# Two broadcast VectorE products and three ScalarE products per output tile in place of eight and eight

## The chip, the core and the metric

The kernel runs on one core of a Trainium2 chip. The metric is the device time of one execution in microseconds (us); lower is better. Three parts of the core matter here: VectorE (DVE in the profile) and ScalarE (ACT), which do the arithmetic, and the 16 DMA engines, which move data between the chip's main memory (HBM) and the on-chip memory (SBUF). DMA transfers are issued from the instruction queue of SyncE (SP) and from the one of ScalarE; each of the two has its own DMA queue, q1 for SP and q10 for ScalarE.

## The reference

Each token's row of 512 numbers is written out twice, once multiplied by its first weight and once by its second. The expert indices are not used.

```python
batch, seq, hidden = x.shape            # 16, 1024, 512, float32
k = expert_indices.shape[-1]            # 2
x_expanded = x[:, :, np.newaxis, :].repeat(k, axis=2)
weights = expert_weights[..., np.newaxis]
return (x_expanded * weights).astype(np.float32)
```

So 33.5 MB are read, 67.1 MB are written, and there is one multiplication for each number written.

## The kernel before, in words

The 16384 tokens are cut into 8 groups of 2048. A group lies in SBUF as one x_tile of 128 partitions with 16 tokens each (4096 KB), so that each partition reads one contiguous stretch of 32 KB. The x pool has two buffers (line 41). A group's results fill two output tiles, o_tile, of 8 tokens by 2 weights by 512 numbers (4096 KB each); the output pool has four buffers (line 42). All weights lie in one w_tile of 128 partitions by 256 numbers.

Lines 54 and 55 issue eight small loads of weights from SP, one for each group. The function load (lines 69 to 77) issues the 4096 KB load of one x_tile from ScalarE's queue (line 76). Lines 79 and 80 load groups 0 and 1; after group i has been worked on, line 109 asks for group i + 2, which takes the buffer of group i and therefore has to wait until every product that reads it is done.

The loop over the 8 tokens of an output tile makes two products for each token: weight 1 on ScalarE (lines 91 to 95) and weight 0 on VectorE (lines 97 to 103). Each reads 512 numbers in each partition and multiplies them by one weight per partition. After the eighth token SP issues the store of the whole o_tile (lines 105 to 108). A store waits for both engines' products; a product into a recycled o_tile waits until the store of four output tiles earlier has landed.

Waits between engines and the order of instructions in each engine's queue are made by the Tile framework: it orders an engine's instructions itself, so that a load's place in ScalarE's queue need not be the place of its line in the source. In the trace the load of line 76 stands in ScalarE's queue behind the first product of the next group. Below, stores and output tiles are counted from 0 to 15, groups and their loads from 0 to 7.

Of the kernel before, what the change touches and what calls it, by code (L numbers as in the profile page):

```python
# [1 line left out]

# [4 lines left out]


@with_exitstack
def kernel(  # L10
    ctx: ExitStack,
    tc: tile.TileContext,
    x: bass.AP,
    expert_indices: bass.AP,
    expert_weights: bass.AP,
    out: bass.AP,
):
    nc = tc.nc

    batch, seq, hidden = x.shape  # L20
    k = expert_weights.shape[-1]
    P = nc.NUM_PARTITIONS
    ntok = batch * seq
    assert ntok % P == 0
    A_TOTAL = ntok // P

    f32 = mybir.dt.float32
    row = k * hidden
    TX = 16
    TO = 8  # L30


    groups = [[16], [16], [16], [16], [16], [16], [16], [16]]
    assert sum(sum(g) for g in groups) == A_TOTAL

    xf = x.rearrange("b s h -> (b s) h")
    of = out.rearrange("b s k h -> (b s) (k h)")
    wf = expert_weights.rearrange("b s k -> (b s) k")

    w_pool = ctx.enter_context(tc.tile_pool(name="w_pool", bufs=1))  # L40
    x_pool = ctx.enter_context(tc.tile_pool(name="x_pool", bufs=2))
    o_pool = ctx.enter_context(tc.tile_pool(name="o_pool", bufs=4))

    w_tile = w_pool.tile([P, A_TOTAL * k], f32)

    def rows(of_all, done, T):
        return of_all[done * P : (done + T) * P, :].rearrange(
            "(p a) n -> p (a n)", a=T
        )

    weights = []
    for group in groups:
        weights.append((sum(n for _, n in weights), sum(group)))
    for at, T in weights:
        nc.sync.dma_start(out=w_tile[:, at * k : (at + T) * k], in_=rows(wf, at, T))

    tiles = []
    done = 0
    for group in groups:
        T = sum(group)  # L60
        a0 = 0
        for n in group:
            tiles.append((done, T, a0, n))
            a0 += n
        done += T

    loaded = []

    def load(i):
        if i >= len(tiles):  # L70
            return
        done, T, a0, n = tiles[i]
        x_tile = x_pool.tile([P, TX * hidden], f32)
        cols = rows(xf, done, T)[:, a0 * hidden : (a0 + n) * hidden]
        for lo, hi in [(0, P)]:
            nc.scalar.dma_start(out=x_tile[lo:hi, : n * hidden], in_=cols[lo:hi, :])  # L76
        loaded.append(x_tile)

    for i in range(2):
        load(i)  # L80
    for i, (done, T, a0, n) in enumerate(tiles):
        x_tile = loaded[i]
        outr = rows(of, done, T)
        for t in range(n):
            if t % TO == 0:
                o_tile = o_pool.tile([P, TO * row], f32)
            for kk in range(k):
                c = (done + a0 + t) * k + kk
                o = t % TO * row + kk * hidden
                if kk == 1:  # L90
                    nc.scalar.mul(  # L91
                        out=o_tile[:, o : o + hidden],
                        in_=x_tile[:, t * hidden : (t + 1) * hidden],
                        mul=w_tile[:, c : c + 1],
                    )
                    continue
                nc.vector.tensor_scalar(  # L97
                    out=o_tile[:, o : o + hidden],
                    in0=x_tile[:, t * hidden : (t + 1) * hidden],
                    scalar1=w_tile[:, c : c + 1],  # L100
                    scalar2=None,
                    op0=mybir.AluOpType.mult,
                )
            if (t + 1) % TO == 0:
                nc.sync.dma_start(
                    out=outr[:, (a0 + t + 1 - TO) * row : (a0 + t + 1) * row],
                    in_=o_tile,
                )
        load(i + 2)

# [1 line left out]
_INS = ['x', 'expert_indices', 'expert_weights']  # L112
_OUTS = [((16, 1024, 2, 512), 'float32')]


# [23 lines left out]
```

## Time and profile before

| | |
|---|---|
| median of 5 runs | 240.12 us (240.06 to 240.21) |
| the profiled execution's own time | 240.09 us |
| its span, first to last instruction | 238.3 us |
| VectorE busy | 52.0 us in 128 instructions, mean 481 ns |
| ScalarE busy | 81.3 us, of which 80.1 us are 128 products, mean 708 ns |
| bytes over DMA | 100.81 MB, mean 423 GB/s |
| a store, from issue to landing | 21.6 to 57.1 us, median 48.4 us |
| a load of x, from issue to landing | 12.5 to 23.3 us, median 23.2 us |
| a load of weights, from issue to landing | 3.9 to 22.3 us, median 21.0 us |

The time lies 1.8 us above the span: work around the program that the trace of the program does not contain. A DMA's issue is only its order; its packets run later, and it counts as landed when the last of them has arrived. A row of instructions gives the engine, the operation, output and inputs, the shape, the count, the busy time and the mean of one; "idle before" is how long the engine stood still before such instructions, and what ended it. A row of a stretch of time gives its length, the busy time of each engine with the number of instructions begun in it, the clock of TensorE (not used here), the mean busy share of the 16 DMA engines and their rate. Packets are counted at their start, so in short stretches a share can lie above 1.

### The profile page before, as it was taken

How to read it: one execution, taken by the hardware profiler on the slowest of the kernel's cores; microseconds unless marked ns; L12 is line 12 of the kernel's file. 1: busy time of each engine (PE TensorE's matmuls, PEld its weight loads, DVE VectorE, ACT ScalarE, POOL GpSimd, SP SyncE). 2: the span in 40 equal slices, each digit the busy share in tenths (PEclk: the TensorE clock that was granted, in tenths of full speed). 3: DMA queues.
4: the chain of work that ended last, by engine and by line, in shares of the span. 5: the costliest groups of instructions: out<-in, count | busy, mean ns of one | idle time of the engine just before them, and what ended most of it. 6: DMA issues, size and time to landing. Idle time of an engine off the chain costs nothing.

```text
span 238.3 us, 384 instructions
## 1 busy us (share of the span) xinstructions
DVE 52.0 (22%) x128; ACT 81.3 (34%) x129; POOL 0.2 (0%) x4
## 2 busy tenths in 40 slices
DVE  0073900045005004050230503214040235000000
ACT  1079960076107007080260803417043256200000
POOL 0000000000000000000000000000000000000000
DMA  6999999999999999999999999999999999999996
GB/s 267 442 442 362 435 435 424 413 424 429 440 440 440 437 440 440 435 429 429 429 418 429 429 440 440 440 435 440 440 435 424 435 429 418 429 429 440 440 440 264
DMA packets 4610, 100.81 MB, mean 423 GB/s; under 512 B 1536, under 2 KB 1536, under 8 KB 1536
## 3 DMA queue, kind: packets, MB, share of 16 engines
q1 hardware_dynamic: 3456, 67.24, 65.6%
q10 hardware_dynamic: 1152, 33.55, 33.1%
q14 instruction: 2, 0.02, 0.0%
HBM read 33.69 MB, written 67.11 MB: 423 GB/s over the span
## 4 chain that ended last, share of the span: by engine, by line
DMA 60%; another core or an unknown queue 12%; ACT 12%; ACTq 1%; issue 0%
DMA out_dram<-o_tile 41%; DMA x_tile<-in_x_dram 18%; ACT o_tile L91 12%; DMA w_tile<-in_expert_weights_dram 2%; ACTq L76 0%; ACTq L134 0%; ACTq L91 0%
## 5 line engine op out<-in xcount | busy, mean ns | idle before, releaser
L91 ACT ACTIVATE o_tile<-x_tile,w_tile 128x512 f32<-128x512 f32 x128 | 80.1, 708 | 117.4 <-DMA out_dram<-o_tile 96.3
L97 DVE TENSOR_SCALAR o_tile<-x_tile,w_tile 128x512 f32<-128x512 f32 x128 | 52.0, 481 | 150.2 <-DMA out_dram<-o_tile 115.7
L91 ACT ACT_TABLE_LOAD x1 | 1.3, 1283 | 5.0 <-DMA w_tile<-in_expert_weights_dram 5.0
L123 POOL MEMSET const-bfloat16-1.0<- 128x1 bf16 x1 | 0.1, 101 | 0.0
L123 POOL MEMSET const-uint8-127<- 128x1 uint8 x1 | 0.1, 101 | 0.0
L123 POOL MEMSET const-float32-0.0<- 128x1 f32 x1 | 0.1, 98 | 0.2 <-issue 0.2
L123 POOL MEMSET const-float32-1.0<- 128x1 f32 x1 | 0.1, 98 | 0.0
## 6 DMA issues: line engine op xcount, KB each, us to landing
out_dram<-o_tile SPq DMA_DIRECT2D x16, 4096.0 KB, 48.4
x_tile<-in_x_dram ACTq DMA_DIRECT2D x8, 4096.0 KB, 23.2
w_tile<-in_expert_weights_dram SPq DMA_DIRECT2D x8, 16.0 KB, 21.0
```

Of the source, the lines that this page charges most:

```text
L91: nc.scalar.mul(out=o_tile[:, o : o + hidden], in_=x_tile[:, t * hidden : (t + 1) * hidden], mul=w_tile[:, c : c + 1],)
L97: nc.vector.tensor_scalar(out=o_tile[:, o : o + hidden], in0=x_tile[:, t * hidden : (t + 1) * hidden], scalar1=w_tile[:, c : c + 1], scala ...
L123: nc = _bacc.Bacc("TRN2", target_bir_lowering=False, num_devices=1)
```

## The change

The products of one output tile are given out differently. Of the 16 products (8 tokens, 2 weights), VectorE takes both weights of tokens 0 to 4 in one instruction of 5120 numbers per partition, and weight 0 of tokens 5 to 7 in a second one of 1536. Both are products of two tensors: x is read with a broadcast over the weights, and the weights with a broadcast over the 512 numbers. ScalarE keeps weight 1 of tokens 5 to 7, three products in the same form as before. Over the 16 output tiles VectorE has 32 instructions in place of 128, ScalarE 48 products in place of 128; in numbers per partition, VectorE goes from 4096 to 6656 for each output tile, ScalarE from 4096 to 1536. Loads, stores, tiles and buffers stay as they are.

```diff
     w_tile = w_pool.tile([P, A_TOTAL * k], f32)
+    ws = w_tile.rearrange("p (a k) -> p a k", k=k)
...
-        for t in range(n):
-            if t % TO == 0:
-                o_tile = o_pool.tile([P, TO * row], f32)
-            for kk in range(k):
-                c = (done + a0 + t) * k + kk
-                o = t % TO * row + kk * hidden
-                if kk == 1:
-                    nc.scalar.mul(...)
-                    continue
-                nc.vector.tensor_scalar(...)
+        xs = x_tile.rearrange("p (t h) -> p t h", h=hidden)
+        for t0 in range(0, n, TO):
+            o_tile = o_pool.tile([P, TO * row], f32)
+            os = o_tile.rearrange("p (t k h) -> p t k h", k=k, h=hidden)
+            c0 = done + a0 + t0
+
+            def product(t, kk):
+
+                m, s = t.stop - t.start, kk.stop - kk.start
+                nc.vector.tensor_tensor(
+                    out=os[:, t, kk, :],
+                    in0=xs[:, t0 + t.start : t0 + t.stop, :]
+                    .unsqueeze(2)
+                    .to_broadcast([P, m, s, hidden]),
+                    in1=ws[:, c0 + t.start : c0 + t.stop, kk]
+                    .unsqueeze(3)
+                    .to_broadcast([P, m, s, hidden]),
+                    op=mybir.AluOpType.mult,
+                )
+
+            split = TO - 3
+            product(slice(0, split), slice(0, k))
+            product(slice(split, TO), slice(0, k - 1))
+            for t in range(split, TO):
+                o = t * row + (k - 1) * hidden
+                c = (c0 + t) * k + k - 1
+                nc.scalar.mul(
                     out=o_tile[:, o : o + hidden],
-                    in0=x_tile[:, t * hidden : (t + 1) * hidden],
-                    scalar1=w_tile[:, c : c + 1],
-                    scalar2=None,
-                    op0=mybir.AluOpType.mult,
+                    in_=xs[:, t0 + t, :],
+                    mul=w_tile[:, c : c + 1],
                 )
-            if (t + 1) % TO == 0:
-                nc.sync.dma_start(
-                    out=outr[:, (a0 + t + 1 - TO) * row : (a0 + t + 1) * row],
-                    in_=o_tile,
-                )
+            nc.sync.dma_start(
+                out=outr[:, (a0 + t0) * row : (a0 + t0 + TO) * row], in_=o_tile
+            )
         load(i + 2)
```

More of the change, by code (lines that the diff above doesn't have):

```diff
@@ L83 @@
         outr = rows(of, done, T)
-        for t in range(n):
-            if t % TO == 0:
-                o_tile = o_pool.tile([P, TO * row], f32)
-            for kk in range(k):
-                c = (done + a0 + t) * k + kk
-                o = t % TO * row + kk * hidden
-                if kk == 1:
[L91 to L94, printed above, removed]
-                    )
-                    continue
-                nc.vector.tensor_scalar(
+        xs = x_tile.rearrange("p (t h) -> p t h", h=hidden)
@@ L98 @@
                     out=o_tile[:, o : o + hidden],
-                    in0=x_tile[:, t * hidden : (t + 1) * hidden],
-                    scalar1=w_tile[:, c : c + 1],
-                    scalar2=None,
-                    op0=mybir.AluOpType.mult,
-                )
-            if (t + 1) % TO == 0:
-                nc.sync.dma_start(
-                    out=outr[:, (a0 + t + 1 - TO) * row : (a0 + t + 1) * row],
-                    in_=o_tile,
-                )
+                    in_=xs[:, t0 + t, :],
```

## The prediction

> **What bounds the kernel now.** I read first the page's busy times, its row of DMA shares and its table of DMA queues.
>
> ```profile
> DVE 52.0 (22%) x128; ACT 81.3 (34%) x129; POOL 0.2 (0%) x4
> ...
> DMA  6999999999999999999999999999999999999996
> ...
> q1 hardware_dynamic: 3456, 67.24, 65.6%
> q10 hardware_dynamic: 1152, 33.55, 33.1%
> ```
>
> The arithmetic engines are a quarter and a third busy. The two DMA queues together fill 65.6 + 33.1 = 98.7% of 16 engines for 238.3 us, that is 235.2 us. Only 3.1 us of the span are without DMA work. The next view says where they are: busy time, DMA share and rate by stretch.
>
> ```profile
> 0.00:2.00 2.00, 0.00 (x0) 0.00 (x0) 0.20 (x4) 1.00 0.40 104
> 2.00:4.00 2.00, 0.00 (x0) 0.00 (x0) 0.00 (x0) 1.00 0.73 281
> 4.00:20.00 16.00, 6.43 (x16) 8.00 (x12) 0.00 (x0) 1.00 1.01 434
> 20.00:24.00 4.00, 0.24 (x1) 3.44 (x7) 0.00 (x0) 1.00 1.07 334
> 24.00:48.00 24.00, 6.87 (x18) 10.42 (x18) 0.00 (x0) 1.00 1.01 434
> ...
> 160.21:204.00 43.79, 13.04 (x32) 20.04 (x32) 0.00 (x0) 1.00 1.01 436
> 204.00:236.00 32.00, 0.00 (x0) 0.00 (x0) 0.00 (x0) 1.00 1.00 432
> 236.00:238.30 2.30, 0.00 (x0) 0.00 (x0) 0.00 (x0) 1.00 0.00 0
> ```
>
> The missing time is in the first 4 us (1.2 + 0.5 us), before any product can start, and in the last 2.3 us, after the last packet has started. In between the share is 1. The rate of 334 GB/s in 20 to 24 us is no idle stretch either: there the queue of SP works off the weights, which come in packets of 128 bytes. So the kernel is bound by DMA from end to end, at 432 GB/s, 9.7 us for each 4096 KB.
>
> Third, the waits: who waited for whom.
>
> ```profile
> DVE o_tile L97 <- DMA out_dram<-o_tile: 115.7, 11, 13.8
> ACT o_tile L91 <- DMA out_dram<-o_tile: 96.3, 11, 12.0
> DVE o_tile L97 <- DMA x_tile<-in_x_dram: 34.5, 3, 17.1
> ACT o_tile L91 <- DMA x_tile<-in_x_dram: 21.1, 3, 13.6
> ```
>
> Columns: who waited for what, us in all, times, the longest. Both engines stand still until a store has freed an output buffer, 11 times, and until x is there, three times: arithmetic waits for DMA. Last, the timeline at the start, the one place where DMA does depend on the products.
>
> ```profile
> 13.29 9.91 ACT L91 ACTIVATE o_tile<-x_tile,w_tile 128x512 f32<-128x512 f32 x16 [6.96 <-DMA x_tile<-in_x_dram]
> 13.29 6.43 DVE L97 TENSOR_SCALAR o_tile<-x_tile,w_tile 128x512 f32<-128x512 f32 x16 [13.29 <-DMA x_tile<-in_x_dram]
> ```
>
> x of group 0 lands at 13.27 us. Store 0 is issued at 18.33 us, when ScalarE's first eight products (5.01 us) are done.
>
> **The change, part by part.** *ScalarE loses five of eight products.* Three take 5.01 x 3/8 = 1.9 us. That is worth nothing: a store waits for the later engine, and this is now VectorE.
>
> *VectorE gets two large instructions for eight small ones.* The trace has no product of two tensors. Its nearest rows bound it. From below: VectorE's own products took 3.26 us for eight, 0.407 us each, so 13 products' worth of numbers take 5.3 us if two tensors stream as fast as one. From above: ScalarE's row, 706 ns for each 512 numbers, times 13 is 9.2 us. [...]
>
> *Store 0* goes out 2.2 us later, at 13.29 + 7.2 = 20.5 us. What hides this? SP's DMA queue works in order, and until about 23 us it is held by the weights: each DMA engine alternates between a 32 KB packet of x (q10) and one 128-byte packet of weights (q1), so the weights end only after x of group 1. In the DMA view, 22.0 to 22.5 us shows no packet of either queue, 22.5 to 23.0 us shows 37 small ones of q1, and 23.0 to 23.5 us is this:
>
> ```profile
> q1 hardware_dynamic: 634, 0.37, 234.3%
> ```
>
> 0.37 MB is more than 634 small packets can hold: nine packets of 32 KB are in it, the first of store 0. So store 0, issued at 18.33, moved nothing before 23.0 us. How early must it be issued? The first load of x was issued at 0.72 us, and no packet started before 1.7 us: about 1 us. Store 0 is therefore in time if issued by about 22.0 us, that is if VectorE takes no more than 8.7 us. At 7.2 us the cost is 0, with 1.5 us in hand; at the lower end 0; at the upper end (9.2 us, issue at 22.5, packets at 23.5 us) up to 0.5 us. If the cover were gone, the 2.2 us would be paid in full.
>
> *Store 1 and load 2.* Both wait for VectorE's second tile: 13.29 + 14.4 = 27.7 us, in place of 24.16 and 24.02 us. Store 0 alone gives 9.7 us of work from 23.2 to 32.9 us, so DMA does not run dry: cost 0, with 4 us in hand after the 1 us of start. Stores 2 and 3 follow at 34.9 and 42.1 us; by then store 1 and load 2 add 19.4 us of work, to 52 us.
>
> *Steady state.* In each group DMA moves three transfers of 9.7 us, 29 us (the trace: products of a new group at 102.2, 131.2, 160.2 us). Products need 2 x 7.2 = 14.4 us of that. When a product may start because a store has landed, three later stores are still pending, 29 us of work for q1, so taking 7.2 instead of 5 us can't empty it. Cost 0; the cover fails only above 14.5 us per tile.
>
> *The load of line 76* has a queue to pass: ScalarE's. Before, it stands behind the first product of the next group, and so waits for an output buffer: tile 7 was done at 93.8 us, but load 5 went out at 102.25 us. Afterwards it waits for VectorE (the last reader of x) and may stand ahead of the next products, or behind up to six of them. In the first case it is issued up to 8.4 - 2.2 = 6 us earlier, in the second up to one tile's turn (14.5 us) later. Late means that q1 has the engines to itself meanwhile; three stores are pending, and a load needs two turns of 9.7 us. Neither adds or removes bytes, and neither empties q1. Cost 0 in both.
>
> *The end.* The last output buffer comes free at 198.8 us; the last store is issued at 203.84 and lands 33.7 us later, behind three others. Issued at 206 it lands at the same 237.5 us; it has some 22 us in hand.
>
> Sum: 238.3 + 0 us of span, and 1.8 us around it: 240.1 us, the profiled execution's own time, 0.03 us under the median of the runs.
>
> **The rivals.** *Slower: store 0 comes late.* If VectorE takes longer than 8.7 us for the first tile, every us above it is a us without DMA, once. [...] For it: nothing in the profile shows this operation. [...] 0.15.
>
> *Slower by traffic.* VectorE would move more through SBUF for twice as long; a 1% loss of DMA rate is 2.3 us (242.4). Against: the stretches with products (436 GB/s) and without (432) show none now. 0.07.
>
> *Faster: loads freed from the wait behind a product* (above), with a gain of what DMA still loses between its first and last packet. 235.2 us of packets, 1.7 at the start and about 1.1 behind the last landing (237.5, and 238.3 the end) leave some 0.3 us: 239.8 us, barely more than nothing. 0.08 for a gain that counts.
>
> [...]
>
> **How the numbers follow.** The main case, no change, has 0.70; its own range is 239.8 to 240.5 us. About 0.2% (0.5 us) is what a measurement of this kernel can tell from no change. Slower has 0.15 + 0.07 = 0.22, faster 0.08. The range goes from 239.7 to 241.3: it takes in a late store of up to 1 us and leaves out the two-cycle product, a real loss of rate, and a gain beyond the idle time that I can find.
>
> **What would show it.** Right: DMA shares of 1 from 4 to 236 us; VectorE's rows near 5.5 and 1.75 us, ScalarE still 706 ns; store 0 issued near 20.5 us, its first packets still at 23 us; the last stores landing 9.7 us apart. Wrong: a stretch without packets between 23 and 28 us, VectorE's sum per tile above 8.7 us, a rate under 432 GB/s while VectorE works, or an empty q1 when a store is issued later on.

## The result and the profile after

The changed kernel takes 242.18 us (median of 24 runs, 240.65 to 243.07) against 240.21 us of the kernel before on the same chip (45 runs). The ratio is 1.0066, 95% interval 1.0051 to 1.0081: slower by 0.66%, some 1.6 us. Over 240.8 us lay 15 of the 45 runs of the kernel before and all but one of the changed kernel; the ratio compares averages and is therefore smaller than the ratio of the medians, 1.0082. The forecast was no change, range 239.7 to 241.3 us. The profiled execution took 242.0 us, with a span of 240.1 us, 1.8 us more than before.

The page of the changed kernel: busy times, DMA share and rate in 40 slices of 6.0 us, the two DMA queues.

```profile
DVE 114.2 (48%) x32; ACT 32.2 (13%) x49; POOL 0.2 (0%) x4
...
DMA  6999999999999999999999999999999999999995
GB/s 265 439 439 436 426 377 437 437 437 431 437 360 431 420 426 437 437 437 437 437 437 437 431 431 388 431 437 433 431 426 426 426 437 431 437 431 437 437 437 235
...
q1 hardware_dynamic: 3456, 67.24, 65.1%
q10 hardware_dynamic: 1152, 33.55, 33.5%
```

The rate in the 40 slices of the kernel before:

```profile
GB/s 267 442 442 362 435 435 424 413 424 429 440 440 440 437 440 440 435 429 429 429 418 429 429 440 440 440 435 440 440 435 424 435 429 418 429 429 440 440 440 264
```

The row of DMA shares is again all nines between the ends: in no slice between them was DMA less than 90% busy. But three slices of the changed kernel's rate (377, 360 and 388) are low; before, one is (362). DMA was busy in them and moved less: packets took longer. The queues say which. Their shares times 16 engines times the span are the time that their packets took. For q1 (stores and weights) that is 0.656 x 16 x 238.3 = 2501 us before and 0.651 x 16 x 240.1 = 2501 us after. For q10 (loads of x) it is 1262 us before and 1287 us after, for the same 1152 packets and bytes. The shares are rounded to 0.1%, so each sum is good to 2 us. The durations of the load packets themselves, added up, are 22.6 us more, 1.4 us for each of the 16 engines. In this trace the stores lost nothing (2485 us of 32 KB packets before and after); the loads of x ran slower.

The rest of the 1.8 us is at the end. In both traces each DMA has 16 packets of 4 bytes, and those of the last store start between 236.9 and 238.9 us, before between 236.3 and 237.2 us. Taken as the ends of the 16 engines, which the trace doesn't name, they lie further apart, and the span lasts until the last of them. The stretch from 237 to 238 us shows it, before and after:

```profile
237.00:238.00 1.00, 0.00 (x0) 0.00 (x0) 0.00 (x0) 1.00 0.00 0
237.00:238.00 1.00, 0.00 (x0) 0.00 (x0) 0.00 (x0) 1.00 0.38 164
```

Where were the loads slow? Busy times, DMA share and rate by stretch, first of the kernel before:

```profile
20.00:24.00 4.00, 0.24 (x1) 3.44 (x7) 0.00 (x0) 1.00 1.07 334
24.00:40.00 16.00, 6.18 (x16) 9.70 (x16) 0.00 (x0) 1.00 0.99 426
64.00:72.00 8.00, 0.00 (x0) 0.00 (x0) 0.00 (x0) 1.00 1.03 442
72.00:144.00 72.00, 16.30 (x40) 25.15 (x40) 0.00 (x0) 1.00 1.00 432
144.00:152.00 8.00, 3.26 (x8) 5.00 (x8) 0.00 (x0) 1.00 1.02 438
152.00:236.00 84.00, 13.04 (x32) 20.04 (x32) 0.00 (x0) 1.00 1.00 433
```

and of the changed kernel:

```profile
20.00:24.00 4.00, 4.00 (x2) 0.72 (x1) 0.00 (x0) 1.00 1.02 391
24.00:40.00 16.00, 16.00 (x6) 3.17 (x5) 0.00 (x0) 1.00 0.99 410
64.00:72.00 8.00, 2.10 (x2) 0.00 (x0) 0.00 (x0) 1.00 1.02 393
72.00:144.00 72.00, 35.80 (x10) 9.73 (x15) 0.00 (x0) 1.00 1.00 433
144.00:152.00 8.00, 0.99 (x1) 1.09 (x2) 0.00 (x0) 1.00 0.97 381
152.00:236.00 84.00, 34.82 (x10) 8.64 (x14) 0.00 (x0) 1.00 1.01 434
```

The last column is the rate. 64 to 72 us lost (442 - 393) / 442 of 8 us, 0.9 us; 144 to 152 us lost 1.0 us; 24 to 40 us 0.6 us. 20 to 24 us won 0.5 us (there the kernel before has slow load packets of its own, the last ones of load 1, 1.97 us each). In 72 to 144 and 152 to 236 us, with VectorE at work for half of the time, the rates are the same. In the two worst stretches VectorE worked 2.1 and 1.0 us of 8, before the slow packets (it ended at 66.1 us) or after them (it began at 151.0 us), so its traffic isn't what slows these.

Closer, the DMA queues from 66 to 70 us (packets, MB, share of 16 engines), before:

```profile
q1 hardware_dynamic: 35, 1.15, 66.3%
q10 hardware_dynamic: 32, 0.52, 30.6%
```

and after:

```profile
q10 hardware_dynamic: 28, 0.92, 74.5%
q1 hardware_dynamic: 22, 0.33, 19.1%
```

Before, 35 store packets of 32 KB took 66.3% of 16 x 4 us, 1.21 us each, and 16 load packets of 32 KB (with 16 small ones) 30.6%, 1.22 us each. After, 28 load packets took 74.5%: 1.70 us each. In the trace single ones took 1.4 to 2.6 us in place of 1.21 us.

### The profile page after: what moved, and what is told of

Read it like the earlier page. It is cut to its first block, busy times and chain, and to the rows that moved or that the text cites. A ratio compares the mean times of both kernels' runs of the same rounds, so it can differ in the third digit from the quotient of the medians.

```text
span 240.1 us, 208 instructions
## 1 busy us (share of the span) xinstructions
DVE 114.2 (48%) x32; ACT 32.2 (13%) x49; POOL 0.2 (0%) x4
## 3 DMA queue, kind: packets, MB, share of 16 engines
q10 hardware_dynamic: 1152, 33.55, 33.5%
## 4 chain that ended last, share of the span: by engine, by line
DMA 63%; DVE 15%; another core or an unknown queue 5%; issue 3%; DVEq 1%; ACT 0%; SPq 0%; ACTq 0%
DMA out_dram<-o_tile 37%; DMA x_tile<-in_x_dram 26%; DVE o_tile L94 15%; DVEq L144 1%; DVEq L94 0%; ACT o_tile L111 0%; SPq L116 0%; ACTq L77 0%; ACTq L111 0%
## 5 line engine op out<-in xcount | busy, mean ns | idle before, releaser
L94 DVE TENSOR_TENSOR o_tile<-x_tile,w_tile 128x5120 f32<-128x5120 f32 (+1 forms) x32 | 114.2, 3621 | 93.6 <-DMA out_dram<-o_tile 58.8
L111 ACT ACTIVATE o_tile<-x_tile,w_tile 128x512 f32<-128x512 f32 x48 | 30.9, 710 | 164.3 <-DMA out_dram<-o_tile 105.8
```

What stands on the lines that cost most here:

```text
L94: nc.vector.tensor_tensor(out=os[:, t, kk, :], in0=xs[:, t0 + t.start : t0 + t.stop, :] .unsqueeze(2) .to_broadcast([P, m, s, hidden]), in ...
L111: nc.scalar.mul(out=o_tile[:, o : o + hidden], in_=xs[:, t0 + t, :], mul=w_tile[:, c : c + 1],)
```

## The experiments

**What differs besides VectorE.** Two moments had moved, and both were in the prediction. First, the start: stores 0 and 1 and load 2 were issued at 20.26, 27.31 and 27.32 us (before: 18.33, 24.16, 24.02). Second, the place of the loads in ScalarE's queue: loads 2 and 3 still stand behind the next group's first product, but loads 4 to 7 ahead of it. In the timeline of the changed kernel:

```profile
66.18 0.36 ACTq L77 DMA_DIRECT2D x_tile<-in_x_dram  x1
77.22 1.95 ACT L111 ACTIVATE o_tile<-x_tile,w_tile 128x512 f32<-128x512 f32 x3 [21.60 <-DMA x_tile<-in_x_dram]
```

Load 4 goes out at 66.18 us, as soon as VectorE has ended group 2 and while load 3 is still under way (it lands at 77.2 us); before, it went out at 72.7 us. The theories: A, these moments make the loads slow; B, VectorE's two-tensor products do, by their traffic; C, a disturbance from outside. Every kernel below was timed beside the kernel before.

| kernel | median us | ratio to before, 95% interval |
|---|---|---|
| changed, once more | 242.05 | 1.0068 (1.0046 to 1.0089) |
| form alone | 240.03 | 0.9993 (0.9974 to 1.0012) |
| split alone | 241.57 | 1.0059 (1.0035 to 1.0083) |
| split, slowed to 7.2 us | 242.06 | 1.0067 (1.0046 to 1.0088) |
| changed, loads behind | 240.98 | 1.0022 (1.0008 to 1.0036) |
| split alone, loads behind | 241.46 | 1.0046 (1.0026 to 1.0066) |
| changed, loads later | 241.04 | 1.0011 (0.9998 to 1.0025) |
| changed, but group 0 as before | 240.86 | 1.0036 (1.0013 to 1.0059) |
| changed, both undone | 240.30 | 0.9992 (0.9976 to 1.0009) |
| before, late start | 241.16 | 1.0024 (1.0005 to 1.0043) |
| before, loads ahead | 241.45 | 1.0033 (1.0012 to 1.0055) |
| before, stores in halves | 276.64 | 269.26 to 292.33 us, no interval |
| changed, same rows read | 242.26 | 1.0068 (1.0047 to 1.0089) |
| group 0 as before, loads later | 240.75 | 1.0009 (0.9990 to 1.0028) |

**The changed kernel once more** (no edit).

> The changed kernel once more, unaltered, for a second trace: are the slow load packets of its first trace (32 KB packets of x that take 1.4 to 2.6 us in place of 1.21 us, near 33, 66 to 69 and 146 to 149 us, together 1.4 us more per DMA engine than before) always there, and at the same places? Theory A (the moments at which loads and stores enter the two queues decide): 241.6 to 242.8 us, again 1 us or more of slow load packets, at the same or at other places. Theory B (VectorE's two-tensor products slow the packets that run beside them): 241.6 to 242.8 us, slow packets only while VectorE works. Theory C (a disturbance from outside the core): slow packets at quite other places, and as many in the kernel before.

Ratio 1.0068. The trace has slow load packets again in load 3 (68.2 to 71.1 us) and load 6 (147 to 148 us): nearly the places of the first trace, with VectorE idle. That speaks against B and C.

```profile
20.00:24.00 4.00, 4.00 (x2) 0.72 (x1) 0.00 (x0) 1.00 0.94 335
...
64.00:72.00 8.00, 1.78 (x2) 0.00 (x0) 0.00 (x0) 1.00 0.99 393
...
144.00:152.00 8.00, 0.93 (x1) 1.03 (x2) 0.00 (x0) 1.00 1.00 401
```

Not all of the first trace comes back. Here some store packets are slow too: from 55.5 to 56 us seven of them took 150.7% of 16 x 0.5 us, 1.72 us each, and 20 to 24 us is as slow as before the change.

**The form alone.**

```diff
-            split = TO - 3
-            product(slice(0, split), slice(0, k))
-            product(slice(split, TO), slice(0, k - 1))
+            split = 0
+            product(slice(0, TO), slice(0, k - 1))
```

> The form of the products alone: VectorE makes the eight weight-0 products of a tile in one two-tensor instruction of 4096 numbers (about 4.4 us), ScalarE keeps its eight products (5.0 us) and so still finishes last; loads and stores are issued when they were before. Theory A: as before, 240.0 to 240.6 us. Theory B: slower in the measure of VectorE's two-tensor work, 4096 of 6656 numbers, +1.2 us: 241.2 to 241.6 us.

As before: 0.9993. The group of its VectorE instructions shows the two-tensor product at 4424 ns for 4096 numbers:

```profile
L94 DVE TENSOR_TENSOR o_tile<-x_tile,w_tile 128x4096 f32<-128x4096 f32 x16 | 70.6, 4424 | 133.2 <-DMA out_dram<-o_tile 103.5 <-DMA x_tile<-in_x_dram 29.8
```

B falls: 70.6 us of such products cost nothing while loads and stores keep their moments. But the trace (of a run of 240.64 us) also shows what the moments don't explain. Load packets from 173 to 174.5 us, in the kernel before and here:

```profile
q10 hardware_dynamic: 16, 0.52, 80.9%
q10 hardware_dynamic: 16, 0.52, 107.9%
```

They took 1.21 us each before and 1.62 us here, although every store, and every load from load 2 on, had up to then gone out within 0.5 us of its time before. Such packets can run slow with or without a shift.

**The split alone, and the split slowed to the changed kernel's pace.** Both use single products with a per-partition weight; the second makes five of them twice.

```diff
-            product(slice(0, split), slice(0, k))
-            product(slice(split, TO), slice(0, k - 1))
+            for t in range(TO):
+                for kk in range(k if t < split else k - 1):
+                    o = t * row + kk * hidden
+                    c = (c0 + t) * k + kk
+                    # slowed: the next call twice where kk == 1
+                    nc.vector.tensor_scalar(
+                        out=o_tile[:, o : o + hidden], in0=xs[:, t0 + t, :],
+                        scalar1=w_tile[:, c : c + 1], scalar2=None,
+                        op0=mybir.AluOpType.mult,
+                    )
```

> The split alone: VectorE makes 13 single products with a per-partition weight (13 x 0.407 = 5.3 us), ScalarE three. VectorE finishes last, as in the changed kernel, and the loads follow it, but a tile takes 5.3 us, about as before (5.0 us). Theory A: if the delay of 2.2 us at the start is what matters, as before, 240.0 to 240.6 us; if the place of the load in ScalarE's queue matters, as changed, 241.6 to 242.8 us. Theory B: as before, 240.0 to 240.6 us.

> The timing of the changed kernel without its instructions: as the split alone, but VectorE makes the five weight-1 products twice (the second writes the same numbers over the first), 18 x 0.407 = 7.3 us for each tile, against 7.2 us in the changed kernel. Stores and loads are issued within 0.2 us of the changed kernel's moments. Theory A: 241.6 to 242.8 us. Theory B: as before, 240.0 to 240.6 us.

With 7.2 us per tile (115.1 us of VectorE for 16 tiles) and no two-tensor product at all the loss is that of the changed kernel (1.0067). No two-tensor product is needed for it: A stands. But the trace is not a copy of the changed kernel's: load 3 is slow (397 GB/s from 64 to 72 us), load 6 is not (434 GB/s from 144 to 152 us), and the engines end even further apart, from 236.7 to 239.6 us. The split with 5.2 us per tile (83.6 us for 16) also loses most of the time (1.0059), and there the start is only 0.1 us later (store 0 at 18.45 us); so the first tile's delay of 2.2 us (7.24 us in the changed kernel, 5.01 before) isn't the whole cause. Its slow loads are elsewhere (352 GB/s from 118 to 122 us, before 434), and its last engine ends at 240.2 us, the first at 237.1 us.

**One moment undone at a time.** In the changed kernel the loads are put back behind the next group's first ScalarE product (for "loads later": of the second tile, `t0 == TO`); issue_after fixes the order in the queue: in the first of these traces load 4 goes out at 76.35 us, while that product runs (from 76.27 us, for 0.72 us).

```diff
                     mul=w_tile[:, c : c + 1],
                 )
+                if i > 0 and t0 == 0 and t == split:
+                    with tc.issue_after(nc.cur_bb.bb.instructions[-1]):
+                        load(i + 1)
...
-        load(i + 2)
```

And group 0 is given out as before, with the rest as changed:

```diff
-            split = TO - 3
-            product(slice(0, split), slice(0, k))
+            split = TO - 3 if i > 0 else 0
+            if split:
+                product(slice(0, split), slice(0, k))
             product(slice(split, TO), slice(0, k - 1))
```

> The changed kernel with the place of the load undone: loads 4 to 7 again stand in ScalarE's queue behind the first product of the next group (in the changed kernel they stand ahead of it and go out when VectorE ends the group). VectorE's products, their 7.2 us per tile and the later first stores stay. Theory L (the earlier loads make load packets slow): 240.0 to 240.6 us, as before. Theory S (the later stores and loads at the start decide): 241.6 to 242.6 us, as changed. Both together: between, near 241.

> The changed kernel with group 0 given out as before (eight two-tensor products on VectorE in one instruction, eight on ScalarE), so that stores 0 and 1 and load 2 go out when they did before (18.3, 24.2 and 24.0 us); from group 1 on as changed, loads 4 to 7 ahead of the next group's products. Theory L: 241.4 to 242.4 us. Theory S: 240.0 to 240.6 us.

Neither L (the early loads) nor S (the late start) alone: 1.0022 with the loads undone, 1.0036 with the start undone. Which slow stretch goes with which moment shows in the stretches. The changed kernel with the loads behind (start still late):

```profile
64.00:72.00 8.00, 1.74 (x2) 0.00 (x0) 0.00 (x0) 1.00 1.03 401
...
144.00:152.00 8.00, 4.63 (x1) 1.95 (x3) 0.00 (x0) 1.00 1.02 438
```

With group 0 as before (loads 4 to 7 still ahead):

```profile
64.00:72.00 8.00, 0.00 (x0) 0.00 (x0) 0.00 (x0) 1.00 1.02 442
...
144.00:152.00 8.00, 1.64 (x1) 1.74 (x3) 0.00 (x0) 1.00 1.03 442
```

The late start brings the slow packets of load 3: from 64 to 72 us all seven traces with a late start have 381 to 406 GB/s, and all eight others 434 to 442. The place at 147 us is gone in both: in these traces load 6 ran slow only with late start and early loads together (though the slowed split has both and does not show it). This second trace is of a run of 240.42 us and has next to no slow packets after 24 us; other runs of that kernel went to 243.45 us, and none of these was traced. So where the early loads lose their time is not shown.

> The changed kernel with each load later than in the kernel before: behind the first ScalarE product of the second tile of the next group, up to one tile's turn (14.5 us) later. Theory L in its simple form (the earlier a load, the more it costs): 239.8 to 240.4 us. If it is no matter of early or late but of where a load falls against the stores' ends: anything from 240.5 to 243 us. If a late load starves the products: over 243 us.

0.11%, with an interval that reaches down to nothing (its median lies further off, 0.3% above): later loads are no dearer than loads behind the first product. That early loads cost more the earlier they are isn't shown by this.

> The split alone (13 single VectorE products in 5.3 us, three ScalarE products) with loads 4 to 7 again behind the first product of the next group. The split alone took 241.57 us. Stores come within 0.4 us of the kernel before. Theory L: 240.0 to 240.5 us. If the three ScalarE products or the 0.3 us of delay mattered: 241.2 us or more.

A miss for the simple theory: 1.0046, where as before was expected. In its trace the stores come 0.5 to 1.3 us later than before (store 0 at 18.87, store 3 at 35.05 us against 33.73), its loads in the order of before. Of this 0.4 us is not the edit's: the split alone, with the same products, issued store 0 at 18.45 us. The trace has slow load packets in load 4 (85 to 91 us), and the runs fall in two groups, eight of 22 up to 240.92 us and the rest from 241.35 to 243.15 us. So either a shift much smaller than 2.2 us can be enough, or something else in this split costs; no run here decides it.

**Both undone, and each one added to the kernel before.** Both undone is the two edits above together. The late start in the kernel before is the slowed split in group 0 alone. The early loads in it come from ten single VectorE products and six ScalarE products per tile from group 1 on, so that VectorE ends last.

```diff
-            split = TO - 3
+            split = TO - 3 if i == 0 else 0   # late start: slowed split, loads behind
...
-            split = TO - 3
+            split = 2 if i > 0 else 0         # loads ahead: single products
```

> The changed kernel with both suspects undone: group 0 given out as before (so that stores 0 and 1 and load 2 go out when they did before) and loads 4 to 7 behind the first product of the next group. From group 1 on VectorE's two two-tensor products still take 7.2 us for each tile. Undone one at a time, the two left +0.22% (load undone) and +0.36% (start undone) of the change's +0.66%. If the two make the loss: 240.0 to 240.5 us. If the 7.2 us per tile in later groups or VectorE's traffic count as well: 240.8 us or more.

> The late start alone: the kernel before, but in group 0 VectorE makes 18 single products per tile (five of them twice) and ScalarE three, so that stores 0 and 1 and load 2 go out near 20.6, 27.7 and 27.7 us as in the changed kernel. From group 1 on eight and eight single products, loads behind the next group's first product, all as before. If the late start costs what is left when only the load's place is undone: 240.6 to 241.1 us, with slow load packets of load 3 near 65 to 70 us. If it costs nothing by itself: 240.0 to 240.4 us.

> The early loads alone: the kernel before in group 0; from group 1 on VectorE makes ten single products per tile (4.1 us) and ScalarE six (3.8 us), so that VectorE ends a tile and loads 5 to 7 stand ahead of the next group's first product; a tile takes up to 1 us less than before. If early loads cost by themselves: 240.8 to 241.8 us, with slow load packets after 90 us. If only together with the late start: 240.0 to 240.4 us.

The times of all three are as the theory had them (the late start 0.06 us above its range). Both undone: 0.9992, with the whole of the changed work on VectorE from group 1 on. Its stretches:

```profile
64.00:72.00 8.00, 0.00 (x0) 0.00 (x0) 0.00 (x0) 1.00 1.01 434
72.00:144.00 72.00, 35.80 (x10) 9.73 (x15) 0.00 (x0) 1.00 1.00 432
144.00:152.00 8.00, 5.42 (x2) 1.94 (x3) 0.00 (x0) 1.00 1.02 442
```

VectorE works half of the time, and the rate is the one of before. Stores 2 and 3 of this kernel still go out later than before, at 31.09 and 38.15 in place of 28.83 and 33.73 us, and that costs nothing: a later store is not dear as such. The two added singly to the kernel before cost +0.24% and +0.33%; left over singly in the changed kernel, they cost +0.22% and +0.36%. Their sum, 0.57 or 0.58%, lies within the interval of the change's 0.66%; each of the four is good to 0.2%. In the late start's trace load 3 is slow again, with single products only:

```profile
64.00:72.00 8.00, 0.00 (x0) 0.00 (x0) 0.00 (x0) 1.00 1.03 406
```

The slow packets that were expected after 90 us with the loads ahead are not in that kernel's trace but for a few; it is of its shortest run, 240.51 us.

**Why a load packet is slow.** In the traces many slow load packets stand at a store's end, where the stores' queue shows only packets of 4 bytes. From 33.2 to 34 us of the changed kernel, at the end of store 0, 16 of these stand beside 16 load packets:

```profile
q10 hardware_dynamic: 16, 0.52, 222.3%
q1 hardware_dynamic: 16, 0.00, 1.1%
```

222.3% of 16 x 0.8 us for 16 load packets is 1.78 us each. That load follows load on a DMA engine there was the author's guess, since the trace doesn't name a packet's engine. And not every such place is slow: in the trace of the kernel before, loads go on at 1.21 us a packet at the ends of stores 0, 1, 3, 5, 7 and 9. To double the ends, each store was cut in two:

```diff
-            nc.sync.dma_start(
-                out=outr[:, (a0 + t0) * row : (a0 + t0 + TO) * row], in_=o_tile
-            )
+            for lo in (0, P // 2):
+                nc.sync.dma_start(
+                    out=outr[lo : lo + P // 2, (a0 + t0) * row : (a0 + t0 + TO) * row],
+                    in_=o_tile[lo : lo + P // 2, :],
+                )
```

> Where the slow load packets come from. [...] Here the order of the kernel before (form alone: one two-tensor product of eight rows, eight ScalarE products, loads behind the next group's first product), but each store is two DMAs of 64 partitions, so that there are twice as many stores' ends. If each such end can stall the loads: 240.8 to 242 us, with slow load packets at the new ends. If only certain moments do: 240.0 to 240.5 us.

276.64 us: far off, and no answer. Its page shows why:

```profile
q1 hardware_dynamic: 3712, 67.24, 65.3%
q10 hardware_dynamic: 1152, 33.55, 30.6%
```

With a span of 272.9 us these are 2851 us for the stores (1.39 us a 32 KB packet on average) and 1336 us for the loads (1.30 us). Most packets kept 1.21 us; 19% of the store packets and 17% of the load packets took more than 1.3 us, up to 3.4 us. A new loss among stores, far larger than the one in question, covers whatever the ends do: halving the stores changed more than the number of ends.

Then the addresses: loads 2 to 7 read the rows of groups 0 and 1 again.

```diff
-        cols = rows(xf, done, T)[:, a0 * hidden : (a0 + n) * hidden]
+        cols = rows(xf, tiles[i % 2][0], T)[:, a0 * hidden : (a0 + n) * hidden]
```

> The changed kernel, every instruction and every queue as it is, but loads 2 to 7 read the rows of group 0 or 1 again in place of their own (so the products of groups 2 to 7 use the wrong tokens). Only the HBM addresses of the reads differ. If the slow load packets hang on where in HBM a load reads against where a store writes: another time, 240.0 to 241.3 us or over 243 us, and the slow packets of load 3 near 65 to 70 us gone or elsewhere. If only the moments count: 241.6 to 242.8 us, with slow packets of load 3 at the same place.

No difference, 1.0068, and the slow packets are at the same place. (The products of groups 2 to 7 then use the rows of groups 0 and 1.) From 66 to 70 us:

```profile
q10 hardware_dynamic: 30, 0.98, 78.8%
```

78.8% of 64 us for 30 packets is 1.68 us each. So the rows that the loads read are not what slows them. Where the stores write was not varied.

**A version that might beat both**, with group 0 as before and the loads later:

> A version that might beat both kernels: the changed kernel with group 0 given out as before, and each load later than before, behind the first ScalarE product of the second tile of the next group (in the changed kernel that load cost +0.11%, against +0.22% behind the first tile's product). If later is better or as good: 239.6 to 240.4 us. If each move of the loads away from where the kernel before has them costs: 240.7 to 241.8 us.

1.0009: no different from the kernel before, and not faster.

## Why the prediction was wrong, step by step

*ScalarE and VectorE*: right. The groups of the changed kernel:

```profile
L94 DVE TENSOR_TENSOR o_tile<-x_tile,w_tile 128x5120 f32<-128x5120 f32 x16 | 87.8, 5490 | 93.6 <-DMA out_dram<-o_tile 58.8 <-DMA x_tile<-in_x_dram 34.8
...
L94 DVE TENSOR_TENSOR o_tile<-x_tile,w_tile 128x1536 f32<-128x1536 f32 x16 | 28.0, 1752 | 0.0
```

The forecast reckons with 7.2 us for a tile (5.5 and 1.75 us for its two products), an estimate of the author's that no trace of the kernel before shows; the changed kernel's trace showed 5490 + 1752 = 7242 ns. ScalarE's products took 710 ns (forecast 706). The two-cycle product that the range leaves out is in no run.

*Store 0 hidden behind the weights*: right as to waiting. It was issued at 20.26 us (forecast 20.5), and its first packets came between 22.0 and 22.5 us, with DMA at a share of 1.02 from 20 to 24 us. The weights stood before it in q1 beside x in q10, packet for packet: from 14 to 19 us of the kernel before the two queues show 65 packets each. *Store 1 and load 2, steady state, end*: right as to waiting too; the row of DMA shares is all nines between its ends, and the last stores landed 9.7 us apart (210.2, 219.9, 229.6, 239.2 us).

*The load of line 76*: "Neither adds or removes bytes, and neither empties q1. Cost 0 in both." This failed, and with it "Cost 0" for the late store 0, store 1 and load 2. The premise behind them was that a DMA that is never idle moves 432 GB/s, so that only an empty queue could cost time. The runs show that the same packets take longer or shorter (load packets 1.21 to 2.61 us in the first trace), and more often longer when loads and stores are issued at other moments. Moved loads cost about 0.35%, the moved start about 0.23%, where the sum had 0 for both.

The sign stood in the profile before, and was read wrongly. The prediction put the 334 GB/s of 20 to 24 us down to the weights' packets of 128 bytes. From 20.7 to 21.5 us of the kernel before the loads' queue has this:

```profile
q10 hardware_dynamic: 16, 0.52, 246.5%
```

246.5% of 16 x 0.8 us for 16 packets is 1.97 us each: load packets at 61% of the rate of those of 1.21 us, in a stretch with a DMA share of 1.07. That is 16 x 0.76 us, 0.8 us for each of 16 engines, most of what this stretch lost.

*The size of "no change"*: the prediction took 0.5 us as enough to tell from no change; the five runs known then lay within 0.15 us. The 45 runs span 239.89 to 242.15 us: in a third of its runs the kernel before itself loses about 1 us.

*The rivals.* "Slower: store 0 comes late" was right in naming the start, wrong in its mechanism, which needed idle engines. "Slower by traffic" fell with the form alone and with both undone. The sign that the prediction itself named, a rate under 432 GB/s while VectorE works, was half of it: the rate fell, in the two worst stretches beside an idle VectorE.

What stays open is what slows a load at some stores' ends and not at others. The rows read, VectorE's traffic and its instruction's form are excluded as the cause of this loss; the number of stores' ends was not tested cleanly; why the split with loads behind loses 0.46% is not explained. "Moments" is as far as the runs go, and they change how often packets run slow rather than decide it: the kernel before, unshifted, has runs up to 242.15 us.

## What to carry to other kernels

This DMA-bound kernel lost time with DMA busy (393 GB/s at a share of 1.02 from 64 to 72 us, before 442 at 1.03): read the rate beside the share, turn each queue's share into time per packet to see which transfers have slowed, and look how far apart the last store's 16 small packets lie. An edit to arithmetic with slack to spare still moved when stores were issued (store 0 from 18.33 to 20.26 us) and where loads stood in an engine's queue (load 4 from 72.7 to 66.18 us). Keep those moments (here: a few tile products given out differently in the first group, and a fixed place for the load), and the edit cost nothing here (0.9992); a forecast of "no change" from full cover needs a margin for transfers that move (here 0.66%).

## What the hardware showed that was not expected

Load packets of 32 KB, 1.21 us each nearly everywhere, took up to 2.6 us, 1.70 us on average over 4 us, while the stores kept 1.21 us in the first trace. The kernel before isn't free of it: the last packets of its load 1 took 1.97 us. All seven traces with a late start lack just these, but in most of them store packets are slow at 22 to 23 us instead, so that the rate from 20 to 24 us is 309 to 391 GB/s there. And cutting each 4096 KB store into two of 64 partitions, with the same 32 KB packets, made the kernel 36 us slower.
